# Scans that take their floor from a PSUM bank, one value accumulator in the first half, and half of a gate sum on ScalarE and POOL

## The chip, the cores and the metric

The kernel runs on one core of one Trainium2 chip. The metric is the device time of one execution in microseconds (us): 707.28 us, the median of three executions (706.64 to 707.72). Everything is fp32 at the interface. On the chip each matrix operand is split into a high and a low part (fp32r), and a product is made of three matmuls.

## The reference

One layer: adaptive LayerNorm of x (1024 x 1024), one projection into two groups of eight heads of 64, attention of two kinds, a SiLU gate, an output projection, and a residual with LayerNorm whose gate comes from a vector `c`. The two parts that the change touches:

```python
mod = jax.nn.silu(c) @ w_ada[layer] + b_ada[layer]
gate = mod[:, 2 * D_MODEL:]                      # the residual gate, 1024 numbers
...
def _stick_breaking_block(q, k, v, q_pos, k_pos):
    z = jnp.einsum('bhqd,bhkd->bhqk', q, k).astype(jnp.float32) * scale
    strict = k_pos[None, :] < q_pos[:, None]
    log_beta = jax.nn.log_sigmoid(z)
    log_keep = jnp.where(strict, jax.nn.log_sigmoid(-z), 0.0)
    later = lax.cumsum(log_keep, axis=3, reverse=True) - log_keep
    w = jnp.where(strict, jnp.exp(log_beta + later), 0.0)
    return jnp.einsum('bhqk,bhkd->bhqd', w.astype(v.dtype), v)
```

In words: the weight of key k for query q is sigmoid(z) at k times the product of sigmoid(-z) over the keys between k and q. The other group (forgetting attention) is an ordinary causal softmax.

## The kernel before, in words

**Stages.** The start (to about 96 us) normalises x, turns it (transposes on PE into PSUM tiles `xT`), and makes q, k and the gate `sg` for the first head pairs with accumulators `acc0` (first half of the columns) and `acc1` (second half); in between, `gate_term` (L690) sums the residual gate on VectorE (DVE): `gate += wg[kt] * sc[:, kt]`, eight terms, each in two halves of 512 columns. From 96 us on the attention runs over eight head pairs p = 0 to 7. Pairs 0 to 3 are stick-breaking, pairs 4 to 7 are softmax. A unit (p, h, i) is one head h and one block i of 128 queries against its `ke = (i + 1) * 128` keys. A pair has 16 units; in pairs 0 to 3 the block runs upward from 0 to 7 for each head, in pairs 4 to 6 downward, and in pair 7 the two heads alternate. Each unit goes through `att_scores` (S on PE at L410 and L411), two units later `att_transpose` (T on PE at L456, split into a high and a low part on ScalarE, L458, and DVE, L459), and after every second unit `att_pv` (L464), the product with the values. The next head pair's projections (`m`, L256 to L258; `v`, L311 to L313) are spread between the units as fillers. The tail is the output projection (`o`).

**A stick-breaking unit** in `att_scores`: ScalarE (ACT) makes `kp` = sigmoid(-S) and `be` = sigmoid(S) (L429, L430); the S tile has a single buffer, so the next unit's S waits for both. DVE then runs two scans from right to left over `kp`. A scan keeps a state: at each element, state = (data0 * state) op1 data1. The first (L434) goes over the 128 columns of the diagonal block with data1 = `ident` and op1 = max: the 1 of the identity starts the product at the diagonal, and its zeros keep what lies right of it at zero. The second (L437) goes over the `ke - 128` columns left of it, with data0 and data1 both `kp`, op1 = min, and starts from the last state. POOL multiplies `be` by the shifted `kp` (L439). Both scans read two streams from SBUF.

**The accumulators of `att_pv`.** `pv_tile` (L65) has two PSUM buffers with one tag, which all 64 products take in turn. After a product ACT copies one half of the rows (L490), DVE adds the other (L491), and POOL multiplies by the gate (L492).

**What sets the order.** PE's instructions stand in the order in which the program is written, and in the start SyncE's (SP) too. On DVE, ACT and POOL a scheduler orders instructions when the program is built; on the chip each engine then works through its own list in order. `after(...)` only holds a scheduled instruction behind others. [...]

Of the kernel before, what the change touches and what calls it, by code (L numbers as in the profile page):

```python
# [8 lines left out]
F32 = mybir.dt.float32  # L9
F32R = mybir.dt.float32r  # L10
AF = mybir.ActivationFunctionType
ALU = mybir.AluOpType

P = 128
# [13 lines left out]
def tile_hybrid_layer(  # L28
# [33 lines left out]
    def acc_tile(name):  # L62
        return ps.tile([P, 512], F32, tag="acc", bufs=2, name=name)

    def pv_tile(name):  # L65
        return ps.tile([P, 512], F32, tag="pv", bufs=2, name=name)

    def t_tile(name):
        return ps.tile([P, 512], F32, tag="T", bufs=2, name=name)
# [306 lines left out]


    st_w, st_pt = {}, {}

    zq = {}  # L380
    turn = [0, 0]
# [15 lines left out]
    def att_scores(u, following):  # L397
        p, h, i = u
        z = zq.pop(u)
        ke = (i + 1) * P  # L400
        ns = 1 if ke <= 512 else 2
        w = ke // ns
        qs = slice(i * P, i * P + P)
        dg = slice(ke - P, ke)
        if p >= 4:
            f = fb[2 * (p - 4) + h]
        S = s_tile(f"S_{p}_{h}_{i}")
        for s in range(ns):
            ks = slice(s * w, s * w + w)
            nc.tensor.matmul(S[:, s, :w], qst[p][h][:, qs], kst[p][h][:, ks], start=True, stop=False)  # L410
            nc.tensor.matmul(S[:, s, :w], z, klo[p][:, ks], start=False, stop=True)  # L411
        v3 = lambda a: a[:, :ke].rearrange("p (a b) -> p a b", a=ns)
        if p >= 4:
            a = att_tile(f"a_{p}_{h}_{i}")
            nm = sb.tile([P, 1], F32, tag="nm", bufs=4, name=f"nm_{p}_{h}_{i}")
            l = sb.tile([P, 1], F32, tag="l", bufs=4, name=f"l_{p}_{h}_{i}")
            nc.vector.tensor_tensor_reduce(out=v3(a), in0=S[:, :ns, :w], in1=v3(f),  # L417
                                           op0=ALU.add, op1=ALU.min, scale=-1.0, scalar=BIG,
                                           accum_out=nm)
            if following:  # L420
                att_causal(following)
            nc.scalar.activation(a[:, :ke], a[:, :ke], AF.Exp, scale=-1.0, bias=nm, accum_out=l)  # L422
            nc.vector.reciprocal(l, l)  # L423
            nc.gpsimd.tensor_scalar(a[:, :ke], a[:, :ke], l, 1.0, op0=ALU.mult, op1=ALU.mult)  # L424
            st_w[u] = a
        else:
            kp = att_tile(f"kp_{p}_{h}_{i}")
            be = att_tile(f"be_{p}_{h}_{i}")
            nc.scalar.activation(v3(kp), S[:, :ns, :w], AF.Sigmoid, scale=-1.0)  # L429
            nc.scalar.activation(v3(be), S[:, :ns, :w], AF.Sigmoid)  # L430


            rv = kp[:, dg][:, ::-1]
            nc.vector.tensor_tensor_scan(rv, rv, ident[:, ::-1], initial=0.0, op0=ALU.mult, op1=ALU.max)  # L434
            if i:
                rv = kp[:, :ke - P][:, ::-1]
                nc.vector.tensor_tensor_scan(rv, rv, rv, initial=kp[:, ke - P:ke - P + 1],  # L437
                                             op0=ALU.mult, op1=ALU.min)
            nc.gpsimd.tensor_tensor(be[:, :ke - 1], be[:, :ke - 1], kp[:, 1:ke], op=ALU.mult)  # L439
            nc.gpsimd.memset(be[:, ke - 1:ke], 0.0)  # L440
            st_w[u] = be
# [20 lines left out]
    y_last = []  # L462

    def att_pv(p, h, j):  # L464
        acc = pv_tile(f"pv_{p}_{h}_{j}")
        last = 2 * j + 1

        def product(part, kb, m=P, start=False, stop=False):
            pt = st_pt[p, h, j, kb // 4][part]
            q0 = P if kb == last else 0  # L470
            nc.tensor.matmul(acc[:m, q0:256], vt[p][:, kb, h * P:h * P + m], pt[:, kb % 4, q0:],  # L471
                             start=start, stop=stop)

        for kb in range(max(1, last - 1)):
            product(0, kb, start=kb == 0)
        product(0, last)
        for kb in range(last - 1):
            product(1, kb, HD)  # L480
        product(1, last, HD)
        if j:
            product(1, last - 1, HD)
        product(0 if j else 1, last - 1, stop=True)
        r = slice(h * HD, h * HD + HD)
        o = slice((1 - h) * HD, (1 - h) * HD + HD)
        qs = slice(j * 256, j * 256 + 256)
        ty = sb.tile([P, 512], F32, tag="ty", bufs=2, name=f"ty_{p}_{h}_{j}")
        tm, yt = ty[:, :256], ty[:, 256:]
        nc.scalar.copy(tm[r, :], acc[o, :256])  # L490
        nc.vector.tensor_tensor(yt[r, :], acc[r, :256], tm[r, :], op=ALU.add)  # L491
        nc.gpsimd.tensor_tensor(yt[r, :], yt[r, :], sgt[p][r, qs], op=ALU.mult)  # L492
        if p == NPAIR - 1:
            if not y_last:
                y_last.extend([big("sg", 2, "y7h", F32R), big("kl", 2, "y7l", F32R)])
            yh, yl = y_last
            nc.scalar.copy(yh[r, qs], yt[r, :])
            nc.gpsimd.tensor_tensor(yl[r, qs], yt[r, :], yh.bitcast(F32)[r, qs], op=ALU.subtract)
        else:
            nc.sync.dma_start(y_dr[p, r, qs], yt[r, :])  # L500
# [15 lines left out]
    START = ((0, 0), (0, 1), (0, 2), (1, 0), (1, 1))  # L516
    NW = 4
    xt_early = t_tile("xT_early")
    acc0 = [t_tile("st_q0"), acc_tile("st_k0"), acc_tile("st_g0"), pv_tile("st_q1"), pv_tile("st_k1")]
    raw_w, split, split_at, used = {}, {}, {}, [0]  # L520
    raws = []

# [167 lines left out]
    def gate_term(kt, h):  # L690
        s = slice(h * 512, h * 512 + 512)
        if kt == 0:
            nc.vector.tensor_scalar(gate[:, s], wg[kt][:, s], sc[:, 0:1], None, op0=ALU.mult)
        else:
            nc.vector.scalar_tensor_tensor(gate[:, s], wg[kt][:, s], sc[:, kt:kt + 1], gate[:, s],
                                           op0=ALU.mult, op1=ALU.add)
# [34 lines left out]
    for kb in range(NB):  # L731
# [5 lines left out]
        if kb < len(evacs):  # L737
            n, h = evacs[kb]
            with after(*rounded):
                evac_m(*START[n], 0, acc0[n], (h,))  # L740
    acc1 += [pv_tile("st_g0b"), pv_tile("st_q1b"), acc_tile("st_k1b")]
    v0_w.update((n, fetch_w(f"v0_{n}b", w_v[0, n], 512)) for n in (2, 3))
    for n in range(5):
        if n >= 2:
            for kb in range(NB):
                start_steps((n,), acc1, kb, 512, 1024)
                step = (n - 2) * NB + kb
                if step % 3 == 1 and step // 3 < GEARLY:
                    with after(rounded[1]):
                        gate_term(step // 3, 0)  # L750
                        gate_term(step // 3, 1)
                    if step // 3 < 4:
                        load_gate(step // 3 + 4)
        last_evac = evac_m(*START[n], 1, acc1[n])
    bf_sb = cp.tile([P, 8], F32, tag="bf", name="bf_sb")
    nc.sync.dma_start(bf_sb, b_f.to_broadcast([P, 8]))
    start_order.__exit__(None, None, None)
# [279 lines left out]
```

## Time and profile before

| | before |
|---|---|
| median of 3 runs | 707.28 us |
| the profiled execution's own time | 706.96 us |
| its span in the profile | 705.2 us |
| granted TensorE clock, mean | 0.997 |
| PE, DVE, ACT, POOL busy | 678.0, 513.8, 378.6, 421.6 us |

"Busy" is the time in which an engine had an instruction; an idle time is put down to the instruction that released the engine (the releaser). The views used below are the page's groups, the groups by shape, the waits of one engine, the timeline of one engine (start, duration, engine, line, names; in brackets the idle time before the row and its releaser) and a table by stretch. 1.76 us of the execution's time lie outside the span.

### The profile page before, as it was taken

Reading aid. Unit: us, or ns where it says so; the run is one execution under the profiler, and the core shown is the slowest. Engines: PE = TensorE matmul, PEld = TensorE weight load, DVE = VectorE, ACT = ScalarE, POOL = GpSimd, SP = SyncE. Lnnn points to the kernel's source line nnn. Section 1 sums busy time; section 2 is a strip of 40 time slices with the busy share of each in tenths; the row PEclk is TensorE's granted clock in tenths of the full one; section 3 lists DMA queues with packets and bytes.
Section 4 is the critical chain, followed back from the end, with each engine's and each line's share of the span. In section 5 each row is a group of like instructions: output and inputs, shape, how many; then the busy total and the mean of one; then the engine's idle time right before and its main releaser. Section 6 shows DMA issues by size and latency. Waiting matters only on the chain.

```text
span 705.2 us, 11790 instructions
## 1 busy us (share of the span) xinstructions
PE 678.0 (96%) x4033; PEld 589.7 (84%) x4033; DVE 513.8 (73%) x963; ACT 378.6 (54%) x856; POOL 421.6 (60%) x523
## 2 busy tenths in 40 slices
PE   7999998989999999999999999999999999999995
PEld 4789887878898888889988887889988889888884
DVE  5985689897858697788686684759576767784644
ACT  4667346756658566666665554645564667621000
POOL 4560258665629675857368898858574455665412
PEclk9999999999999999999999999999999999999998
DMA  8953451102101212112044654435251189143301
GB/s 306 416 211 126 128 172 35 28 26 53 53 7 36 71 37 68 42 38 68 9 124 126 201 162 131 148 104 170 71 170 53 56 268 374 43 159 122 121 32 59
DMA packets 44027, 81.59 MB, mean 116 GB/s; under 512 B 5120, under 2 KB 18880, under 8 KB 43072
## 3 DMA queue, kind: packets, MB, share of 16 engines
q1 hardware_dynamic: 42816, 76.65, 32.9%
q10 hardware_dynamic: 1152, 4.19, 2.1%
q8 instruction: 32, 0.52, 0.3%
q14 instruction: 27, 0.22, 0.1%
HBM read 60.34 MB, written 16.29 MB: 109 GB/s over the span
## 4 chain that ended last, share of the span: by engine, by line
PE 54%; DVE 3%; POOL 3%; DMA 2%; issue 1%; ACT 1%; POOLq 0%; SPq 0%; DVEq 0%; ACTq 0%
PE pv L471 6%; PE m L256 6%; PE m L257 6%; PE m L258 6%; PE T L456 6%; PE o L825 4%; PE o L823 4%; PE o L824 4%; PE S L410 3%; PE S L411 3%; PE v L311 2%; PE v L313 2%; PE v L312 2%; DMA fb<-f_dr 1%; DVE kp L437 1%
## 5 line engine op out<-in xcount | busy, mean ns | idle before, releaser
L256 PE MATMUL m<-uh,whi 128*128 128x512 f32 x304 | 126.3, 416 | 0.8 <-DVE kl L244 0.8
L257 PE MATMUL m<-ul,whi 128*128 128x512 f32 x304 | 119.8, 394 | 0.0
L258 PE MATMUL m<-uh,wlo 128*128 128x512 f32 x304 | 119.6, 394 | 0.0
L459 DVE TENSOR_TENSOR pt<-T,pt 128x512 fp32r<-128x512 f32 (+2 forms) x192 | 100.5, 549 | 14.8 <-ACT pt L458 13.5
L439 POOL TENSOR_TENSOR be<-be,kp 128x127 f32<-128x127 f32 (+3 forms) x64 | 79.1, 1236 | 48.6 <-DVE kp L437 45.9
L458 ACT CAST pt<-T 128x512 fp32r<-128x512 f32 (+2 forms) x192 | 85.7, 480 | 18.7 <-PE T L456 15.3
L471 PE MATMUL pv<-pt,v 128*128 128x256 f32 (+3 forms) x640 | 82.9, 273 | 6.2 <-DVE pt L459 5.4
L471 PEld LDWEIGHTS pv<-pt,v 128*128 128x128 f32 (+1 forms) x640 | 77.6, 163 | 12.5 <-DVE pt L459 7.1
L437 DVE TENSOR_TENSOR_SCAN kp<-kp 128x128 f32<-128x128 f32 (+6 forms) x56 | 83.0, 1483 | 1.9
L424 POOL TENSOR_SCALAR a<-a,l 128x1024 f32<-128x1024 f32 (+3 forms) x64 | 48.4, 756 | 41.7 <-DVE l L423 29.5
L422 ACT ACTIVATE a<-a,nm 128x1024 f32<-128x1024 f32 (+3 forms) x64 | 49.8, 778 | 40.0 <-DVE nm L417 39.2
L410 PE MATMUL S<-k,q 128*128 128x512 f32 (+5 forms) x192 | 66.6, 348 | 2.4 <-ACT be L430 1.7
L258 PEld LDWEIGHTS m<-uh,wlo 128*128 128x128 f32 x304 | 57.1, 188 | 13.5
L411 PE MATMUL S<-kl,qz 128*128 128x512 f32 (+5 forms) x192 | 65.5, 342 | 0.0
L256 PEld LDWEIGHTS m<-uh,whi 128*128 128x128 f32 x304 | 57.3, 188 | 9.6 <-DVE kl L244 1.2
L257 PEld LDWEIGHTS m<-ul,whi 128*128 128x128 f32 x304 | 57.4, 189 | 7.9
L434 DVE TENSOR_TENSOR_SCAN kp<-kp,ident 128x128 f32<-128x128 f32 x64 | 42.5, 665 | 24.6 <-ACT kp L429 22.9
L492 POOL TENSOR_TENSOR ty<-ty,sg 64x256 f32<-64x256 f32 x64 | 49.3, 771 | 18.5 <-DVE ty L491 8.8
L429 ACT ACTIVATE kp<-S 128x128 f32<-128x128 f32 (+3 forms) x64 | 41.7, 652 | 32.2 <-PE S L411 30.7
L417 DVE CUSTOM_DVE_ANT_0 a<-S,fb 128x1024 f32<-128x1024 f32 (+3 forms) x64 | 48.3, 754 | 14.5 <-PE S L411 5.9
L126 POOL TENSOR_TENSOR wlo<-raw,whi 128x512 fp32r<-128x512 f32 x38 | 56.6, 1492 | 2.4 <-DMA wo_dr<-wlo_o 0.8
L311 PE MATMUL v<-whi_v,uh 128*128 128x256 f32 (+1 forms) x192 | 56.1, 292 | 1.2 <-DVE kl L244 1.2
(280 smaller groups left out, 1637.5 us busy)
## 6 DMA issues: line engine op xcount, KB each, us to landing
raw<-in_w_qkg_dram SPq DMA_DIRECT2D x38, 256.0 KB, 3.0
wss<-in_w_ss_dram SPq DMA_DIRECT2D x7, 1024.0 KB, 8.3
x<-in_x_dram SPq DMA_DIRECT2D x8, 512.0 KB, 7.7
k<-k SPq DMA_DIRECT2D x32, 128.0 KB, 2.2
wg<-in_w_gate_dram SPq DMA_DIRECT2D x8, 512.0 KB, 5.0
raw_o<-in_w_out_dram SPq DMA_DIRECT2D x16, 256.0 KB, 2.7
fb<-f_dr ACTq DMA_DIRECT2D x8, 512.0 KB, 4.3
wo_dr<-whi_o SPq DMA_DIRECT2D x16, 256.0 KB, 2.8
```

Of the source, the lines that this page charges most:

```text
L126: nc.gpsimd.tensor_tensor(lo[:, :n], raw, hi.bitcast(F32)[:, :n], op=ALU.subtract)
L256: nc.tensor.matmul(acc, hi[:, c], u_hi[kt][:, s], start=(kt == 0), stop=False)
L257: nc.tensor.matmul(acc, hi[:, c], u_lo[kt][:, s], start=False, stop=False)
L258: nc.tensor.matmul(acc, lo[:, c], u_hi[kt][:, s], start=False, stop=(kt == NB - 1))
L311: nc.tensor.matmul(acc[:, :n], u_hi[kt][:, ts_], hi[:, s], start=(kt == 0), stop=False)
L410: nc.tensor.matmul(S[:, s, :w], qst[p][h][:, qs], kst[p][h][:, ks], start=True, stop=False)
L411: nc.tensor.matmul(S[:, s, :w], z, klo[p][:, ks], start=False, stop=True)
L437: nc.vector.tensor_tensor_scan(rv, rv, rv, initial=kp[:, ke - P:ke - P + 1], op0=ALU.mult, op1=ALU.min)
L439: nc.gpsimd.tensor_tensor(be[:, :ke - 1], be[:, :ke - 1], kp[:, 1:ke], op=ALU.mult)
L458: nc.scalar.copy(hi[:, :n, qo:qo + P], t3)
L459: nc.vector.tensor_tensor(lo[:, :n, qo:qo + P], t3, hi.bitcast(F32)[:, :n, qo:qo + P], op=ALU.subtract)
L471: nc.tensor.matmul(acc[:m, q0:256], vt[p][:, kb, h * P:h * P + m], pt[:, kb % 4, q0:], start=start, stop=stop)
```

## The change

Four edits. A PSUM bank with the tag `fl` holds a tile `floor` during the first half: zeros in columns 0 to 383 and the identity in columns 384 to 511 (written once, at the end of the start, by DVE and ACT). The scans of a unit take data1 from it: one scan of up to 512 columns that covers the diagonal block and the blocks left of it, and, where `ke` is over 512, a second one over the rest whose data1 is the first column of `floor`, broadcast (zeros), with op1 = max. The bank comes from the second `pv` buffer: `att_pv` has one buffer in pairs 0 to 3, and from pair 4 on the two banks in turn by j. In pair 7, where the heads alternate, two products that follow each other then have the same j and so the same bank. The accumulators of the start that took two `pv` buffers take `pv` and `fl`. Last, the first term of the residual gate goes to ACT, and for the first 512 columns of the other seven ACT scales the weight tile in place and POOL adds it to `gate`; the second 512 columns stay on DVE. Both are now held behind both instructions of `rounded`.

```diff
-    def pv_tile(name):
-        return ps.tile([P, 512], F32, tag="pv", bufs=2, name=name)
+    def pv_tile(name, other=False):
+        return ps.tile([P, 512], F32, tag="fl" if other else "pv", bufs=1, name=name)
...
-            rv = kp[:, dg][:, ::-1]
-            nc.vector.tensor_tensor_scan(rv, rv, ident[:, ::-1], initial=0.0, op0=ALU.mult, op1=ALU.max)
-            if i:
-                rv = kp[:, :ke - P][:, ::-1]
-                nc.vector.tensor_tensor_scan(rv, rv, rv, initial=kp[:, ke - P:ke - P + 1],
-                                             op0=ALU.mult, op1=ALU.min)
+            n = min(ke, 512)
+            rv = kp[:, ke - n:ke][:, ::-1]
+            nc.vector.tensor_tensor_scan(rv, rv, floor[0][:, 512 - n:][:, ::-1], initial=0.0,
+                                         op0=ALU.mult, op1=ALU.max)
+            if ke > n:
+                rv = kp[:, :ke - n][:, ::-1]
+                nc.vector.tensor_tensor_scan(rv, rv, floor[0][:, 0:1].to_broadcast([P, ke - n]),
+                                             initial=kp[:, ke - n:ke - n + 1], op0=ALU.mult, op1=ALU.max)
...
-        acc = pv_tile(f"pv_{p}_{h}_{j}")
+        acc = pv_tile(f"pv_{p}_{h}_{j}", p >= 4 and j % 2 == 1)
...
-    acc0 = [t_tile("st_q0"), acc_tile("st_k0"), acc_tile("st_g0"), pv_tile("st_q1"), pv_tile("st_k1")]
+    acc0 = [t_tile("st_q0"), acc_tile("st_k0"), acc_tile("st_g0"), pv_tile("st_q1"), pv_tile("st_k1", True)]
...
         if kt == 0:
-            nc.vector.tensor_scalar(gate[:, s], wg[kt][:, s], sc[:, 0:1], None, op0=ALU.mult)
+            nc.scalar.activation(gate[:, s], wg[kt][:, s], AF.Copy, scale=sc[:, 0:1])
+        elif h == 0:
+            nc.scalar.activation(wg[kt][:, s], wg[kt][:, s], AF.Copy, scale=sc[:, kt:kt + 1])
+            nc.gpsimd.tensor_tensor(gate[:, s], gate[:, s], wg[kt][:, s], op=ALU.add)
         else:
             nc.vector.scalar_tensor_tensor(gate[:, s], wg[kt][:, s], sc[:, kt:kt + 1], gate[:, s],
                                            op0=ALU.mult, op1=ALU.add)
...
-    acc1 += [pv_tile("st_g0b"), pv_tile("st_q1b"), acc_tile("st_k1b")]
+    acc1 += [pv_tile("st_g0b", True), pv_tile("st_q1b"), acc_tile("st_k1b")]
...
-                    with after(rounded[1]):
+                    with after(*rounded):
                         gate_term(step // 3, 0)
                         gate_term(step // 3, 1)
...
+        if n == 2:
+            floor.append(ps.tile([P, 512], F32, tag="fl", bufs=1, name="floor"))
+            nc.vector.memset(floor[0][:, :512 - P], 0.0)
+            nc.scalar.copy(floor[0][:, 512 - P:], ident)
```

What the change moves on the engines is seen at three places. In these lists a row is line, operation, output<-inputs and size of the output; a scan is listed there as SCALAR_TENSOR_TENSOR. PE's order is the same before and after, and DVE's differs only where scans and gate terms come and go.

The first place is DVE at the end of the start. `q` and `kl` are evacuations of the start's accumulators `st_q1b` and `st_k1b`, `wg_831` to `wg_872` the weight tiles of the gate's last four terms. Before:

```order
L695 SCALAR_TENSOR_TENSOR gate<-wg_831,sc,gate 128x512 x2
L695 SCALAR_TENSOR_TENSOR gate<-wg_844,sc,gate 128x512
L233 SCALAR_TENSOR_TENSOR q_0_251<-st_q1b,q_0_251 64x512
L695 SCALAR_TENSOR_TENSOR gate<-wg_844,sc,gate 128x512
L695 SCALAR_TENSOR_TENSOR gate<-wg_857,sc,gate 128x512
L233 SCALAR_TENSOR_TENSOR q_1_252<-st_q1b,q_1_252 64x512
L695 SCALAR_TENSOR_TENSOR gate<-wg_857,sc,gate 128x512
L695 SCALAR_TENSOR_TENSOR gate<-wg_872,sc,gate 128x512 x2
L244 TENSOR_TENSOR kl_255<-st_k1b,k_0_253 64x512
```

The same place on DVE after the change (the weight tiles are numbered 831, 845, 859 and 878 there):

```order
L763 MEMSET floor 128x384
L701 SCALAR_TENSOR_TENSOR gate<-wg_831,sc,gate 128x512
L701 SCALAR_TENSOR_TENSOR gate<-wg_845,sc,gate 128x512
L233 SCALAR_TENSOR_TENSOR q_0_251<-st_q1b,q_0_251 64x512
L701 SCALAR_TENSOR_TENSOR gate<-wg_859,sc,gate 128x512
L233 SCALAR_TENSOR_TENSOR q_1_252<-st_q1b,q_1_252 64x512
L701 SCALAR_TENSOR_TENSOR gate<-wg_878,sc,gate 128x512
L244 TENSOR_TENSOR kl_255<-st_k1b,k_0_253 64x512
```

Ahead of `kl` stand one gate term where there were three; four of eight terms in this stretch left DVE, and the memset of `floor` came.

The second place is POOL over the same time and into the first units. `whi` and `wlo` are the splits of the weights of the fillers, `be` the product of a unit. Before:

```order
L125 TENSOR_SCALAR whi_2_0_1217<-raw_2_0_1215 128x512
L126 TENSOR_TENSOR wlo_2_0_1218<-raw_2_0_1215,whi_2_0_1217 128x512
L125 TENSOR_SCALAR whi_2_1_1223<-raw_2_1_1221 128x512
L126 TENSOR_TENSOR wlo_2_1_1224<-raw_2_1_1221,whi_2_1_1223 128x512
L440 MEMSET be_0_0_941 128x1
L439 TENSOR_TENSOR be_0_0_941<-be_0_0_941,kp_0_0_940 128x127
```

After the change, on POOL:

```order
L699 TENSOR_TENSOR gate<-gate,wg_831 128x512
L699 TENSOR_TENSOR gate<-gate,wg_845 128x512
L699 TENSOR_TENSOR gate<-gate,wg_859 128x512
L125 TENSOR_SCALAR whi_2_0_1224<-raw_2_0_1222 128x512
L699 TENSOR_TENSOR gate<-gate,wg_878 128x512
L125 TENSOR_SCALAR whi_2_1_1230<-raw_2_1_1228 128x512
L126 TENSOR_TENSOR wlo_2_0_1225<-raw_2_0_1222,whi_2_0_1224 128x512
L126 TENSOR_TENSOR wlo_2_1_1231<-raw_2_1_1228,whi_2_1_1230 128x512
L443 MEMSET be_0_0_951 128x1
L442 TENSOR_TENSOR be_0_0_951<-be_0_0_951,kp_0_0_950 128x127
```

Four additions stand ahead of the first unit's `be` that were not on POOL before (three more stand further ahead).

The third place is DVE in two units of the first head, blocks 5 and 6. `pt` is the low part of a turned block, `ty` the evacuation of a product. Before:

```order
L434 SCALAR_TENSOR_TENSOR kp_0_5_1124<-kp_0_5_1124,ident 128x128
L437 SCALAR_TENSOR_TENSOR kp_0_5_1124<-kp_0_5_1124 128x640
L708 SCALAR_TENSOR_TENSOR gate<-bg,gate_1146 128x512
L459 TENSOR_TENSOR pt_0_0_1_0_1112<-T_0_3_0_1149,pt_0_0_1_0_1111 128x4x128
L434 SCALAR_TENSOR_TENSOR kp_0_6_1161<-kp_0_6_1161,ident 128x128
L437 SCALAR_TENSOR_TENSOR kp_0_6_1161<-kp_0_6_1161 128x768
```

After the change, on DVE:

```order
L436 SCALAR_TENSOR_TENSOR kp_0_5_1131<-kp_0_5_1131,floor 128x512
L440 SCALAR_TENSOR_TENSOR kp_0_5_1131<-kp_0_5_1131,floor 128x256
L714 SCALAR_TENSOR_TENSOR gate<-bg,gate_1153 128x512
L462 TENSOR_TENSOR pt_0_0_1_0_1119<-T_0_3_0_1156,pt_0_0_1_0_1118 128x4x128
L436 SCALAR_TENSOR_TENSOR kp_0_6_1168<-kp_0_6_1168,floor 128x512
L440 SCALAR_TENSOR_TENSOR kp_0_6_1168<-kp_0_6_1168,floor 128x384
```

The scans keep their places between the same neighbours; 128 + 640 columns became 512 + 256, and units of up to 512 keys have one scan instead of two.

More of the change, by code (lines that the diff above doesn't have):

```diff
@@ L378, in tile_hybrid_layer @@
     st_w, st_pt = {}, {}
+    floor = []
     zq = {}
```

## The prediction

> **What bounds the kernel now.** I read the page's busy times first, then a table by stretch, then the waits of PE.
>
> ```profile
> span 705.2 us, 11790 instructions
> PE 678.0 (96%) x4033; PEld 589.7 (84%) x4033; DVE 513.8 (73%) x963; ACT 378.6 (54%) x856; POOL 421.6 (60%) x523
> 96.00:365.00 269.00, 258.82 (x1667) 231.96 (x1667) 215.57 (x327) 173.23 (x392) 175.10 (x217) 1.00 0.18 51
> ```
>
> PE is the bound: busy 96% of the span at a full clock. The last row is the stick-breaking half, 96 to 365 us; its columns are the length, then the busy time of PE, weight loads, DVE, ACT and POOL, the clock and DMA. The change touches the end of the start and this half. There PE is idle for only 269.00 - 258.82 = 10.2 us, so whatever DVE saves, no more than about that can come back. Who holds PE in that stretch (from 95 us, so that the first wait is whole):
>
> ```profile
> PE pv L471 <- DVE pt L459: 3.7, 6, 1.3
> PE S L410 <- ACT be L430: 1.7, 1, 1.7
> PE T L456 <- POOL wlo_v L126: 1.6, 1, 1.6
> PE T L456 <- DVE pt L459: 1.3, 1, 1.3
> PE v L311 <- DVE kl L244: 1.2, 1, 1.2
> PE pv L471 <- ACT pt L458: 0.7, 1, 0.7
> PE T L456 <- POOL be L440: 0.2, 1, 0.2
> ```
>
> The rows sum to 10.4 us. DVE ends 3.7 + 1.3 + 1.2 = 6.2 us of them directly. A wait is somewhat longer than its row says, because a matmul's end is modelled:
>
> ```profile
> 92.20 0.40 PE L565 MATMUL st_k1b<-uh,hw 128*128 128x512 f32 x1
> 92.44 0.39 PE L568 MATMUL st_k1b<-ul,hw 128*128 128x512 f32 x1
> ```
>
> The second starts 0.24 us after the first, whose row lasts 0.40. So each of the 12 waits hides about 0.16 us more: 1.9 us, and the whole prize is about 12.3 us.
>
> **The scans.** Their durations by line (minimum/median/maximum in ns), beside the DVE operation that splits the turned blocks:
>
> ```profile
> L434 DVE TENSOR_TENSOR_SCAN kp<-kp,ident x64: 406/427/1954, 97.8 to 360.3; 128x128 f32<-128x128 f32 x64
> L459 DVE TENSOR_TENSOR pt<-T,pt x192: 259/608/693, 102.0 to 644.9; 128x512 fp32r<-128x512 f32 x96, 128x128 fp32r<-128x128 f32 x32, 128x256 fp32r<-128x256 f32 x32, 128x384 fp32r<-128x384 f32 x32
> ```
>
> L434 is one shape, and yet lasts from 0.41 to 1.95 us. L459 reads one stream from PSUM and one from SBUF, and in 192 runs never exceeds 0.693 us. What stretches a scan is POOL at work, and POOL is stretched too:
>
> ```profile
> 117.16 2.94 DVE L437 TENSOR_TENSOR_SCAN kp<-kp 128x896 f32<-128x896 f32 x1
> 118.17 3.49 POOL L439 TENSOR_TENSOR be<-be,kp 128x895 f32<-128x895 f32 x1
> 120.02 0.99 DVE L459 TENSOR_TENSOR pt<-T,pt 128x512 fp32r<-128x512 f32 x2
> 120.74 0.99 PE L471 MATMUL pv<-pt,v 128*64 128x256 f32 x7 [1.29 <-DVE pt L459]
> ```
>
> Here the chain is whole: a long scan overlaps POOL's product, the split of T stands behind the scan in DVE's list, and PE waits 1.29 us. The new scans read `kp` from SBUF and data1 from PSUM, two streams of the same kinds as L459's, so I take them undisturbed. Undisturbed scans, and the sums of all of them from the page:
>
> ```profile
> 331.83 0.42 DVE L434 TENSOR_TENSOR_SCAN kp<-kp,ident 128x128 f32<-128x128 f32 x1
> 332.29 0.48 DVE L437 TENSOR_TENSOR_SCAN kp<-kp 128x128 f32<-128x128 f32 x1
> 345.59 1.28 DVE L437 TENSOR_TENSOR_SCAN kp<-kp 128x512 f32<-128x512 f32 x1
> L437 DVE TENSOR_TENSOR_SCAN kp<-kp 128x128 f32<-128x128 f32 (+6 forms) x56 | 83.0, 1483 | 1.9
> L434 DVE TENSOR_TENSOR_SCAN kp<-kp,ident 128x128 f32<-128x128 f32 x64 | 42.5, 665 | 24.6 <-ACT kp L429 22.9 <-ACT qz L388 1.0
> L437 DVE TENSOR_TENSOR_SCAN kp<-kp 128x896 f32<-128x896 f32 x8 | 20.4, 2556 | 0.3
> ```
>
> From 128 to 512 columns an undisturbed scan grows by 0.80 us, 2.08 ns a column. A first scan then takes 0.42, 0.69, 0.95 and 1.22 us for 128 to 512 columns, and a second (it starts from a value in SBUF) 0.48, 0.75, 1.02 and 1.28. Over the eight blocks of a head that is 0.42 + 0.69 + 0.95 + 5 x 1.22 + 0.48 + 0.75 + 1.02 + 1.28 = 11.7 us; times eight heads 93.5 us, where the two rows show 83.0 + 42.5 = 125.5. DVE is relieved of **32 us**, 0.5 us a unit. No row shows a scan fed from PSUM. Its bounds: not cheaper than one column per step of L459 (512 columns in about 0.69 us, so 8 x 6.7 = 53 us over all), not dearer than now, 125.5, unless PSUM feeds it more slowly than it feeds L459 (a rival below). I take 93.5, from the nearest rows. All scans keep their places in DVE's list.
>
> [...]
>
> **The gate's terms.** The first wait of 1.7 us comes from them:
>
> ```profile
> 92.27 3.46 DVE L695 SCALAR_TENSOR_TENSOR gate<-wg,sc,gate 128x512 f32<-128x512 f32 x3
> 95.76 0.68 DVE L244 TENSOR_TENSOR kl<-st_k1b,k 64x512 fp32r<-64x512 f32 x1
> 96.48 0.58 ACT L241 CAST k<-st_k1b 64x512 fp32r<-64x512 f32 x1 [2.83 <-DVE kl L244]
> 97.26 0.27 ACT L430 ACTIVATE be<-S 128x128 f32<-128x128 f32 x1
> 97.58 0.38 PE L410 MATMUL S<-k,q 128*128 128x256 f32 x1 [1.67 <-ACT be L430]
> ```
>
> Three terms (3.46 us) hold `kl` until 95.76, that holds ACT's second copy of k, which holds `be`, and the second unit's S waits. After the change one term stands there, about 1.2 us at this rate. ACT's first copy still ends near 93.45, so `kl` can run at 93.5, ACT's `be` ends near 95.3, and PE, whose fillers last until 95.9, does not wait: **-1.7 us**. What the moved work costs elsewhere:
>
> ```profile
> L123 POOL TENSOR_TENSOR raw_o<-raw_o,gate 128x512 f32<-128x512 f32 x16 | 20.7, 1294 | 8.8 <-DMA raw_o<-in_w_out_dram 8.6
> L552 ACT CAST whi_st<-raws 128x512 fp32r<-128x512 f32 x5 | 2.9, 616 | 1.2 <-DMA raws<-in_w_qkg_dram 1.2
> L695 DVE SCALAR_TENSOR_TENSOR gate<-wg,sc,gate x14: 743/748/1773, 75.3 to 94.0; 128x512 f32<-128x512 f32 x14
> 82.44 0.62 POOL L125 TENSOR_SCALAR whi_v_2b<-raw_v_2b 128x512 fp32r<-128x512 f32 x1 [29.98 <-PE st_q1b L568]
> 87.28 0.59 ACT L232 ACTIVATE q<-st_q1b 64x512 fp32r<-64x512 f32 x1 [4.39 <-PE st_q1b L568]
> 92.57 0.93 POOL L125 TENSOR_SCALAR whi<-raw 128x512 fp32r<-128x512 f32 x1 [6.29 <-DMA raw<-in_w_qkg_dram]
> 98.33 0.41 POOL L439 TENSOR_TENSOR be<-be,kp 128x127 f32<-128x127 f32 x1 [0.64 <-DVE kp L434]
> 99.74 0.27 PE L456 MATMUL T<-ident,be 128*128 128x128 f32 x1
> ```
>
> ACT gets nine instructions of about 0.62 us (L552 has the shape), 5.6 us, in idle time such as the 4.39 us ahead of 87.28; bounds 0.59 and 0.75 us each change nothing there. The floor's two writes (no row shows a memset into PSUM; between 0.1 and 0.7 us, as an L459 of 512 columns) fall before 87 us, where DVE also has nothing to do. POOL gets seven additions at 1.3 us (L123), bounded by 0.74, the cheapest term on DVE, and 3.5 us, the stretched product above. Three fall into the 29.98 us of idle time ahead of 82.44. The gate's last four weight tiles land only shortly before the raw weights that POOL awaits at 92.57, so one addition falls behind that row and delays the two splits and the first `be` with it: 92.57 + 0.9 (split) + 1.3 (addition) + 0.6 + 2 x 1.3 (splits) + 0.5 = 98.5 to 98.7 at the end of `be`, as before. PE wants it at 99.74 - 1.7 = 98.1: a new wait of **+0.5 us**, up to 3 if the additions stretch, nothing if they run at the lower bound.
>
> **One accumulator in the first half.** A product may start only when ACT and DVE have read the one before. The tightest case:
>
> ```profile
> 112.67 0.99 PE L471 MATMUL pv<-pt,v 128*128 128x256 f32 x8
> 115.30 0.40 DVE L491 TENSOR_TENSOR ty<-pv,ty 64x256 f32<-64x256 f32 x1
> 118.70 0.75 PE L471 MATMUL pv<-pt,v 128*128 128x256 f32 x5
> ```
>
> It is read out at 115.70 and the next product begins at 118.70: 3.0 us of slack, and every other product of the timeline leaves more, those of pair 7 too. With scans shorter, DVE's read comes earlier. **0 us**; if it bit, a tenth of a microsecond a product would be 3 us. Behind the waiting product stand T, S and the fillers of the next unit, which is why it would count in full.
>
> **The sum.** Beside the first wait (-1.7 + 0.5): of the 5.0 us in which PE waits for `pt`, four fifths go, since DVE gains 0.5 us a unit cumulatively while it is behind and 0.9 in a long one (3.46 us for the pair at 117 becomes 2.50); -4.0. Of the remaining 3.7 us (`kl`, POOL's split, ACT's `pt`, `be`) I take 60%, because POOL's products start after the scans and are no longer stretched by them, and `kl` stands behind scans, while ACT and the order of POOL's list stay; -2.2. Hidden parts go in the same proportion, 7.4 of 10.4, of 1.9 us: -1.4. Together -8.8 us. The profiled execution took 706.96 us (span 705.2 and 1.76 around it), so 698.2; it lay 0.3 us under the median, so **698.5 us**. The second half keeps its work, starts earlier and is PE-bound.
>
> **Rivals.** (1) *POOL takes over.* The first half's waits move from DVE to POOL: it gets 9 us more just ahead of the attention, and one wait already ends at its split (1.6 us). The first and POOL's waits then stay: half the gain, 4.4 us, 702.9 us. Against it: POOL is idle for 94 of 269 us and mostly waits for scans. [...] (3) *The waits only change their names*, within 0.2% (1.4 us), about what a measurement can tell from no change. (4) *Slower: PSUM feeds a scan more slowly than SBUF.* A unit has (269.00 - 215.57) / 64 = 0.83 us of idle DVE. The longest pair now takes 0.67 + 2.56 = 3.2 us in the mean (L434, and L437 of 896 columns); the rival decides once it costs over 4.0 us, 1.6 times my 2.5. At twice my cost a long unit is 1.0 us over, and 32 long units add some 20 us after the gate's relief: about 720 us. For it only that no row shows such a scan; against it L459, at full rate.
>
> **Chances.** Forecast 0.70; rival 1 0.14; rival 2 0.05; rival 3 0.04; rival 4 0.07. Faster 0.89, same 0.04, slower 0.07. If every wait goes, 12.3 us, the time is 695.0, and 1.5 us more for gaps too short to be listed give the low end, 693.5; rival 1 with a larger POOL price gives the high end, 704.0.
>
> **What would show it.** Right: scans at 0.42 to 1.28 us with a maximum near the median; no product on POOL near 3.5 us; DVE some 35 us less busy; no wait for `be` near 96; PE's idle in the first half down from 10 to about 3 us. Wrong: scans of over 1.3 us for 512 columns (rival 4), or of scattered length (rival 2); PE's waits ended by POOL (rival 1); a product that waits for L491's successor (the accumulator).

## The result, and the profile after

| | before | after |
|---|---|---|
| median | 706.96 us of 4 runs (706.30 to 707.72) | 699.11 us of 4 runs (698.09 to 699.99) |
| the profiled execution, its span | 706.96, 705.2 us | 699.99, 698.2 us |

The ratio is 0.9888, with a 95% interval of 0.9871 to 0.9905: the kernel became 1.1% faster, 7.85 us, and the forecast of 698.5 us lies 0.6 us under the median. The sections behind this one show that its term for the gate nevertheless failed, and that it left out a wait.

First the busy times of the page, then the stick-breaking half in the table by stretch (length; busy time of PE, weight loads, DVE, ACT, POOL; clock; DMA), for the kernel after:

```profile
span 698.2 us, 11781 instructions
PE 676.0 (97%) x4033; PEld 589.0 (84%) x4033; DVE 483.7 (69%) x931; ACT 385.0 (55%) x866; POOL 410.6 (59%) x530
96.00:365.00 269.00, 264.10 (x1710) 237.65 (x1710) 191.15 (x314) 177.94 (x398) 163.06 (x224) 1.00 0.19 51
```

PE's idle time in that stretch fell from 10.2 to 269.00 - 264.10 = 4.9 us. DVE is 30.1 us less busy over the span, and POOL 11.0 us less, though it got seven additions more. The waits of PE from 92 to 365 us, in the kernel after (us in total, times, longest):

```profile
PE pv L474 <- DVE pt L462: 2.0, 2, 1.6
PE T L459 <- POOL be L443: 1.1, 1, 1.1
PE T L459 <- DVE pt L462: 1.0, 2, 0.9
PE S L411 <- ACT be L431: 0.8, 1, 0.8
PE v L311 <- DVE kl L244: 0.7, 1, 0.7
```

Twelve waits of 10.4 us became seven of 5.6. Two of the seven are new: the 1.1 us for POOL's `be`, which the prediction had at 0.5, and one of 1.6 us for `pt`, which it did not have. Three of the prediction's signs came out weaker: PE's idle time (about 3 us forecast), DVE (about 35 us less busy forecast) and the first wait for `be`, which is shorter but not gone.

The scans and POOL's product, by line (ns, minimum/median/maximum), and the scans of one shape (busy us, mean ns), in the kernel after:

```profile
L440 DVE TENSOR_TENSOR_SCAN kp<-kp,floor x32: 479/880/1281, 105.7 to 355.4; 128x128 f32<-128x128 f32 x8, 128x256 f32<-128x256 f32 x8, 128x384 f32<-128x384 f32 x8, 128x512 f32<-128x512 f32 x8
L442 POOL TENSOR_TENSOR be<-be,kp x64: 402/1204/2002, 98.7 to 356.7; 128x127 f32<-128x127 f32 x8, 128x255 f32<-128x255 f32 x8, 128x383 f32<-128x383 f32 x8, 128x511 f32<-128x511 f32 x8
L436 DVE TENSOR_TENSOR_SCAN kp<-kp,floor 128x512 f32<-128x512 f32 x40 | 48.8, 1219 | 25.6 <-ACT kp L430 24.9 <-issue 0.5
L436 DVE TENSOR_TENSOR_SCAN kp<-kp,floor 128x128 f32<-128x128 f32 x8 | 3.3, 410 | 0.0
L436 DVE TENSOR_TENSOR_SCAN kp<-kp,floor 128x512 f32<-128x512 f32 (+2 forms) x64 | 65.2, 1018 | 32.4 <-ACT kp L430 31.4
```

A scan of one shape now has one duration, to 0.02 us within each shape of the two lines: 1.22 us for 512 columns where 1.22 was forecast (1.20 to 1.22 in 40 scans), 0.41 for 128 where 0.42 was (0.40 to 0.42 in 8). All of L436 and L440 together are 65.2 + 28.1 = 93.3 us (28.1 is 32 times the mean of the four forms, 0.88), against a forecast of 93.5. POOL's product, before up to 3.49 us, is never over 2.00. A scan and a product side by side, DVE and then POOL, in the kernel after:

```profile
115.74 1.22 DVE L436 TENSOR_TENSOR_SCAN kp<-kp,floor 128x512 f32<-128x512 f32 x1
117.00 1.28 DVE L440 TENSOR_TENSOR_SCAN kp<-kp,floor 128x512 f32<-128x512 f32 x1
115.61 1.77 POOL L442 TENSOR_TENSOR be<-be,kp 128x895 f32<-128x895 f32 x1
```

The first scan lies wholly inside POOL's product, and neither is stretched: the scan takes the mean of its shape, and the product 1.77 us, where the same 895 columns took 3.49 beside a scan before.

**Where the time came from.** The starts of the S rows cut the first half into stages that repeat from run to run to about 0.1 us outside stage A (where the start differs). A is the first head of pair 0 (from its first S to the first S of the second head), B goes on to the first S of pair 2, C to the second head of pair 4, when the last stick-breaking unit is through. Worked out from those rows for the kernels of this study, one profile each; "rest" is what remains of the span (the start and everything behind C):

| us | A | B | C | A+B+C | rest |
|---|---|---|---|---|---|
| before | 25.9 | 103.9 | 177.9 | 307.7 | 397.5 |
| after | 25.8 | 99.3 | 176.2 | 301.3 | 396.9 |
| scans only | 27.1 | 99.3 | 176.2 | 302.6 | 397.3 |
| gate only | 26.6 | 104.0 | 177.9 | 308.5 | 395.4 |
| one accumulator only | 27.3 | 103.9 | 177.9 | 309.1 | 397.0 |
| smaller first scan | 25.6 | 99.3 | 176.2 | 301.1 | 397.5 |
| second scan from SBUF | 26.5 | 100.6 | 178.2 | 305.3 | 398.6 |
| gate term late | 25.9 | 99.3 | 176.2 | 301.5 | 395.9 |
| logarithms late | 25.6 | 99.3 | 174.5 | 299.3 | 396.4 |
| `be` first | 24.4 | 99.3 | 176.2 | 299.9 | 397.1 |
| both | 24.3 | 99.3 | 174.5 | 298.1 | 396.4 |

The change wins 6.4 us in A to C, nothing of it in A, where the gate was to pay. The rest scatters between 395.4 and 398.6 us without regard to the scans; of the 1.5 us of the 7.85 that A to C do not explain, 0.6 lie in it, and 0.9 come from the profiled execution of the change being the slowest of its four. Neither is traced further.

### The profile page after: what moved, and what is told of

The parts are those of the page before. It is cut to its first block, busy times and chain, and to the rows that moved or that the text cites. A ratio compares the mean times of both kernels' runs of the same rounds, so it can differ in the third digit from the quotient of the medians.

```text
span 698.2 us, 11781 instructions
## 1 busy us (share of the span) xinstructions
PE 676.0 (97%) x4033; PEld 589.0 (84%) x4033; DVE 483.7 (69%) x931; ACT 385.0 (55%) x866; POOL 410.6 (59%) x530
## 4 chain that ended last, share of the span: by engine, by line
PE 76%; DVE 7%; DMA 5%; POOL 4%; ACT 4%; issue 3%; SPq 0%; POOLq 0%; DVEq 0%; ACTq 0%
PE pv L474 9%; PE m L256 8%; PE m L257 8%; PE m L258 8%; PE T L459 8%; PE o L835 4%; PE o L833 4%; PE o L834 4%; PE S L412 4%; PE S L411 4%; PE v L311 3%; PE v L313 3%; PE v L312 3%; DMA wss<-in_w_ss_dram 1%; DMA raw<-in_w_qkg_dram 1%
## 5 line engine op out<-in xcount | busy, mean ns | idle before, releaser
L462 DVE TENSOR_TENSOR pt<-T,pt 128x512 fp32r<-128x512 f32 (+2 forms) x192 | 100.6, 550 | 16.1 <-ACT pt L461 14.9
L442 POOL TENSOR_TENSOR be<-be,kp 128x127 f32<-128x127 f32 (+3 forms) x64 | 77.1, 1205 | 34.9 <-DVE kp L440 25.9
L436 DVE TENSOR_TENSOR_SCAN kp<-kp,floor 128x512 f32<-128x512 f32 (+2 forms) x64 | 65.2, 1018 | 32.4 <-ACT kp L430 31.4
L495 POOL TENSOR_TENSOR ty<-ty,sg 64x256 f32<-64x256 f32 x64 | 47.7, 745 | 26.5 <-DVE ty L494 12.5
L389 ACT CAST qz<-q 64x128 fp32r<-64x128 f32 x128 | 37.4, 295 | 31.3 <-PE S L412 30.0
L313 PE MATMUL v<-wlo_v,uh 128*128 128x256 f32 (+1 forms) x192 | 54.2, 282 | 0.0
```

The lines of the kernel that those rows point to most:

```text
L313: nc.tensor.matmul(acc[:, :n], u_hi[kt][:, ts_], lo[:, s], start=False, stop=(kt == NB - 1))
L436: nc.vector.tensor_tensor_scan(rv, rv, floor[0][:, 512 - n:][:, ::-1], initial=0.0, op0=ALU.mult, op1=ALU.max)
L462: nc.vector.tensor_tensor(lo[:, :n, qo:qo + P], t3, hi.bitcast(F32)[:, :n, qo:qo + P], op=ALU.subtract)
```

## The experiments

**1. The scans without the gate.** The change with all gate terms back on DVE, held as they were before:

```diff
-            nc.scalar.activation(gate[:, s], wg[kt][:, s], AF.Copy, scale=sc[:, 0:1])
-        elif h == 0:
-            nc.scalar.activation(wg[kt][:, s], wg[kt][:, s], AF.Copy, scale=sc[:, kt:kt + 1])
-            nc.gpsimd.tensor_tensor(gate[:, s], gate[:, s], wg[kt][:, s], op=ALU.add)
+            nc.vector.tensor_scalar(gate[:, s], wg[kt][:, s], sc[:, 0:1], None, op0=ALU.mult)
```

> The change without its gate part (the eight terms stay on DVE). My theory: the scans' feed carries most of the 7.9 us; the gate part is worth the first wait of 1.7 us less the 0.5 to 1.1 us of POOL's new wait, so this kernel loses 0.6 to 1.5 us of the gain: about 700.2 us, and PE again waits about 1.7 us for be near 96 us. Rival (the gate part is the gain): over 703 us.

699.93 us (6 runs; before 706.64 of 23 on that chip), ratio 0.9901, interval 0.988 to 0.9923. The scans alone carry the gain, as far as the intervals tell. PE's wait for `be` is back, at 1.82 us, and A is 1.2 us longer than before, with PE's clock at 0.50 from 97.53 to 100.92 us behind that wait (see the last section). A is also 1.3 us longer than in the change, though the change waits as long in two parts (0.78 + 1.11 us); what the gate part gains beside the new scans is, in these two profiles, the clock.

**2. The gate without the scans.** The kernel before with the new `gate_term` and its `after` alone.

> The kernel before with the gate part alone. My theory: 0.6 to 1.7 us faster than before, about 705.8 us; scans still scattered up to 2 or 3 us, DVE busy some 5 us less, the waits of PE at 115 to 150 us as before. Rival (the gate part is the gain): 702 us or less.

706.89 us (12 runs), ratio 1.0001, interval 0.9989 to 1.0013: no effect, where 0.6 to 1.7 us were expected. The two waits of PE that matter, in this kernel:

```profile
95.62 0.39 PE L410 MATMUL S<-k,q 128*128 128x256 f32 x1 [0.54 <-ACT be L430]
99.35 0.33 PE L456 MATMUL T<-ident,be 128*128 128x128 f32 x1 [1.42 <-POOL be L440]
```

0.54 + 1.42 = 1.96 us stand where 1.67 stood: the wait moved from ACT's `be` to POOL's.

**3. One accumulator alone.** The kernel before with `pv_tile` of the change and no floor.

> The kernel before with one value accumulator in the first half and the two banks by j later; nothing else. My theory: no difference, within 0.7 us of before, and no product that waits for ACT's or DVE's read of the one before. Rival (the single accumulator costs and the scans pay for it): 1 to 3 us slower.

707.67 us (12 runs), ratio 1.0017, interval 1.0002 to 1.0031. That is 1.0 us more than before, beyond the 0.7 expected. No product waits for an accumulator in the list of waits, and B and C are those of before, 103.9 and 177.9 us. The 1.4 us more in A stand behind a gap of 1.78 us, where PE's clock fell to 0.50 for 3.4 us (last section). The mean clock is under 0.996 in nine of its 12 executions, in eight of the 23 of the kernel before. So the clock carries the difference as far as these figures go; whether the edit lengthens that gap (1.67 us before) is not shown.

**4. Smaller scans from the same bank.** With `n = P` in place of `n = min(ke, 512)` the first scan takes 128 columns only, and the number of scans is that of before; all read PSUM.

> The change with its first scan cut to the 128 columns of the diagonal, as before, and the rest in the second, both fed from PSUM: as many scans as before, undisturbed. My theory (the second stream's place is what counts): within 1 us of the change, 699.1 to 700.0 us, no scan more than a few ns from its median, DVE some 5 us busier than in the change. Rival (fewer instructions are what counts): half the gain lost, 703 us or more.

699.63 us (6 runs), ratio 0.9896, interval 0.988 to 0.9913, like the change. DVE is busy 487.4 us, 3.7 more, and PE's waits are those of the change to 0.3 us. So the gain does not come from fewer or merged scans.

**5. The change again**, beside the next two and on the same chip (before 706.90 of 17 runs).

> The changed kernel itself, for a narrower interval on the chip of the next three: 7.0 to 8.5 us faster than before by every theory.

699.25 us (5 runs), ratio 0.9891, interval 0.9872 to 0.991.

**6. The second scan from SBUF.** The scans keep their number and sizes, but the second one, of 32 units out of 64, reads `kp` as data1 again:

```diff
-                nc.vector.tensor_tensor_scan(rv, rv, floor[0][:, 0:1].to_broadcast([P, ke - n]),
-                                             initial=kp[:, ke - n:ke - n + 1], op0=ALU.mult, op1=ALU.max)
+                nc.vector.tensor_tensor_scan(rv, rv, rv,
+                                             initial=kp[:, ke - n:ke - n + 1], op0=ALU.mult, op1=ALU.min)
```

> The change with its second scan fed from SBUF twice, as before (kp as data1, min); the first keeps its floor in PSUM. The number of scans and their columns are those of the change. My theory: the 32 second scans stretch again beside POOL, up to 2 us, first scans stay at 1.22; 1.5 to 4 us of the gain are lost, about 701.5 us. Rival (fewer and merged scans are the gain): no difference from the change.

705.17 us (12 runs), ratio 0.9977, interval 0.9963 to 0.9991. 5.9 of the 7.65 us that the change gains on that chip are gone, more than expected. The same line and two of PE's waits, in this kernel:

```profile
L440 DVE TENSOR_TENSOR_SCAN kp<-kp x32: 484/1018/2407, 105.9 to 359.5; 128x128 f32<-128x128 f32 x8, 128x256 f32<-128x256 f32 x8, 128x384 f32<-128x384 f32 x8, 128x512 f32<-128x512 f32 x8
116.60 0.63 PE L459 MATMUL T<-ident,be 128*128 128x128 f32 x4 [1.83 <-DVE pt L462]
224.28 0.98 PE L474 MATMUL pv<-pt,v 128*64 128x256 f32 x7 [2.57 <-DVE pt L462]
```

The minimum of L440 stays (484 ns beside 479), its maximum goes from 1281 to 2407, and PE waits longer for DVE's split: 1.83 us at 116.60, where the longest such wait of T is 0.9 in the kernel after, and 2.57 at 224.28. The latter is not a scan's: it is the new wait of 1.64 us, grown because the first of the two small steps of experiment 8 takes 1.93 us here, where 1.23 in the change. That the second stream comes from PSUM is what the gain rests on: with the shapes kept, taking it away in a third of the scans gives most of the gain back. A to C account for 4.0 us of the loss, of which that wait is 0.9. The rest of this profile is 398.6 us, with a wait of 2.24 us at 445 us for POOL, whose list waits 1.45 us for the output weights' transfers at 445.13; whether the edit causes it, one profile does not tell. So how much of the 5.9 us the scans alone cost is not separated.

**7. The last gate term later.** The change with gate term 8 written behind the last evacuation of the start, to take its addition off POOL's list ahead of `be`.

> The change with the gate's eighth term written behind the last evacuation of the start and held behind it. My theory: what is left of the waits near 95 and 98 us (0.8 for be on ACT, 1.1 for be on POOL) comes from that term on DVE and POOL; the first goes and the second shrinks to half or less: 0.8 to 1.4 us faster than the change. Rival (the weight splits on POOL hold the first product anyway): the first wait goes and the second grows by as much; same time as the change.

699.12 us (5 runs), ratio 0.9894, interval 0.9872 to 0.9916: the same. POOL's list in this kernel, and the T that waits:

```profile
94.23 1.21 POOL L125 TENSOR_SCALAR whi<-raw 128x512 fp32r<-128x512 f32 x2
95.39 3.00 POOL L126 TENSOR_TENSOR wlo<-raw,whi 128x512 fp32r<-128x512 f32 x2
98.36 1.26 POOL L699 TENSOR_TENSOR gate<-gate,wg 128x512 f32<-128x512 f32 x1
99.61 0.41 POOL L442 TENSOR_TENSOR be<-be,kp 128x127 f32<-128x127 f32 x1
100.07 0.33 PE L459 MATMUL T<-ident,be 128*128 128x128 f32 x1 [1.74 <-POOL be L443]
```

The scheduler put the addition behind the splits and still ahead of `be`. S waits only 0.26 us now, but T 1.74. So the experiment did not clear POOL's list, and the rival was right that it only renames the wait. The list shows what to move instead: the splits, 1.21 + 3.00 us for the weight "1_2", which PE needs later.

**8. The forget gate's logarithms behind the split.** This goes for the new wait of 1.64 us at 220.85 us. DVE, POOL and PE there, in the kernel after:

```profile
217.69 1.23 DVE L346 SCALAR_TENSOR_TENSOR flf<-fsb,fab 128x64 f32<-128x64 f32 x1 [0.94 <-ACT fab L345]
218.95 1.26 DVE L349 TENSOR_TENSOR_SCAN fsb<-flf,later 128x64 f32<-128x64 f32 x1
220.13 0.99 DVE L462 TENSOR_TENSOR pt<-T,pt 128x512 fp32r<-128x512 f32 x2
216.84 2.00 POOL L442 TENSOR_TENSOR be<-be,kp 128x1023 f32<-128x1023 f32 x1 [0.47 <-DVE kp L440]
218.79 2.51 POOL L126 TENSOR_TENSOR wlo<-raw,whi 128x512 fp32r<-128x512 f32 x2
220.85 0.98 PE L474 MATMUL pv<-pt,v 128*64 128x256 f32 x7 [1.64 <-DVE pt L462]
```

And the same two steps with POOL's rows around them, in the kernel before:

```profile
224.49 0.23 DVE L346 SCALAR_TENSOR_TENSOR flf<-fsb,fab 128x64 f32<-128x64 f32 x1 [0.30 <-ACT fab L345]
224.75 0.60 DVE L349 TENSOR_TENSOR_SCAN fsb<-flf,later 128x64 f32<-128x64 f32 x1
222.40 2.21 POOL L125 TENSOR_SCALAR whi<-raw 128x512 fp32r<-128x512 f32 x1
225.19 2.00 POOL L439 TENSOR_TENSOR be<-be,kp 128x1023 f32<-128x1023 f32 x1
```

Two steps of 64 columns took 0.23 and 0.60 us before, when POOL had been held up by a long scan (896 columns, 2.38 us from 221.82; POOL's cast at 222.40 takes 2.21 us, where 0.62 is the median of its line) and came to its product late. After the change POOL is on time, its two-stream operations run from 216.84 to 221.30 without a break, and the two steps, each with two tiles of SBUF, take 1.23 and 1.26. The first ends at 218.92, 0.08 us after POOL's product; the second at 220.21, about when the first of the two `wlo` is through (218.79 and half of 2.51: 220.05). In experiment 6 the first takes 1.93 us, from 220.42, and again ends 0.08 us after POOL's product (222.27). That POOL stretches them is read from these rows; no kernel gave one of their inputs a place in PSUM. The experiment holds both behind the split:

```diff
-        nc.vector.scalar_tensor_tensor(lf, ff, 0.0, ab, op0=ALU.min, op1=ALU.subtract)
+        for _ in range(FLATE):
+            yield
+        with after(last_split[0]):
+            nc.vector.scalar_tensor_tensor(lf, ff, 0.0, ab, op0=ALU.min, op1=ALU.subtract)
...
-            nc.vector.tensor_tensor(lo[:, :n, qo:qo + P], t3, hi.bitcast(F32)[:, :n, qo:qo + P],
-                                    op=ALU.subtract)
+            last_split[0] = nc.vector.tensor_tensor(lo[:, :n, qo:qo + P], t3,
+                                                    hi.bitcast(F32)[:, :n, qo:qo + P], op=ALU.subtract)
```

> The change, with the two last steps of the forget gate's logarithms (the minimum and the running sum, 64 columns each) put behind the split of T that they stand ahead of on VectorE near 217.7 us. Theory: in the change these two take 1.23 and 1.26 us because they read two tiles of SBUF while POOL multiplies and splits, and the split and PE's product wait behind them; with the split ahead of them, PE's wait of 1.64 us at 220.85 falls under 0.5 us, the two steps still last over 1 us each but nobody waits, and the time is 1.1 to 1.6 us below the change (0.9984 of it or less). Rival: the split waits for T or for ScalarE's copy anyway, so the wait keeps at least 1 us under another name and the time stays within 0.5 us of the change.

697.65 us (4 runs; before 706.14 of 9 on that chip, for the last four experiments), ratio 0.9871, interval 0.9852 to 0.989; the change itself took 699.64 beside it. The 1.99 us are more than the 1.1 to 1.6 expected, and all runs (697.43 to 698.03) lie below those of the change (698.74 to 700.07). DVE in this kernel:

```profile
218.06 1.02 DVE L467 TENSOR_TENSOR pt<-T,pt 128x512 fp32r<-128x512 f32 x2 [1.41 <-ACT pt L466]
219.00 1.07 DVE L353 SCALAR_TENSOR_TENSOR flf<-fsb,fab 128x64 f32<-128x64 f32 x1
220.10 1.28 DVE L354 TENSOR_TENSOR_SCAN fsb<-flf,later 128x64 f32<-128x64 f32 x1
```

The split runs at 218.06 in place of 220.13, PE's wait is gone, and C is 1.7 us shorter. The two steps still take 1.07 and 1.28 us, and nobody waits for them. The overlap was not removed but moved to where it is free, as the theory had it.

**9. `be` ahead of the splits.** The change with POOL's splits of the weight "1_2" held behind the first unit's product:

```diff
+        with after(*(first_be if key[:3] == "1_2" else ())):
+            nc.gpsimd.tensor_scalar(hi[:, :n], raw, 1.0, 1.0, op0=ALU.mult, op1=ALU.mult)
+            nc.gpsimd.tensor_tensor(lo[:, :n], raw, hi.bitcast(F32)[:, :n], op=ALU.subtract)
...
+            held = nc.gpsimd.tensor_tensor(be[:, :ke - 1], be[:, :ke - 1], kp[:, 1:ke], op=ALU.mult)
...
+            if not first_be:
+                first_be.append(held)
```

> The change, with POOL's two weight splits near 93.3 to 98.7 us held behind the first unit's product be. Theory: the wait of 1.11 us for be that the change brought in is POOL's queue (two splits and one gate addition ahead of be); without the splits ahead of it be can run at about 96.5 us, PE's wait at 98.1 goes, and the time is 0.8 to 1.3 us below the change. Rival: the wait only moves on: the splits then stand between the first products, the second or third unit's T waits for its be by about as much, and the time stays within 0.5 us of the change.

698.02 us (5 runs), ratio 0.9876, interval 0.9857 to 0.9894; 1.62 us under the change, where 0.8 to 1.3 were expected. POOL's list, in this kernel:

```profile
92.26 3.00 POOL L704 TENSOR_TENSOR gate<-gate,wg 128x512 f32<-128x512 f32 x2 [1.06 <-ACT wg L703]
96.69 0.41 POOL L445 TENSOR_TENSOR be<-be,kp 128x127 f32<-128x127 f32 x1 [0.63 <-DVE kp L439]
97.07 1.20 POOL L126 TENSOR_SCALAR whi<-raw 128x512 fp32r<-128x512 f32 x2
98.86 2.55 POOL L127 TENSOR_TENSOR wlo<-raw,whi 128x512 fp32r<-128x512 f32 x2
```

`be` waits for its scan now, not for POOL, and runs 2 us earlier. T has no wait, A is 24.4 us, 1.4 less than in the change, and no later product waits in its place.

**10. Both.**

> Both of the above in one kernel. Theory: the two waits are apart in time and add: 2 to 2.8 us below the change, a ratio to the kernel before of 0.985 to 0.986. Rival: one of the two does nothing, and the time is that of the other alone.

695.89 us (5 runs, 695.27 to 696.50), ratio 0.9845, interval 0.9825 to 0.9864. The stretch and the waits of PE from 92 to 365 us, in this kernel:

```profile
96.00:365.00 269.00, 266.84 (x1724) 240.17 (x1724) 193.67 (x320) 180.15 (x402) 166.46 (x226) 1.00 0.19 53
PE T L469 <- DVE pt L472: 0.9, 1, 0.9
PE v L315 <- DVE kl L248: 0.7, 1, 0.7
PE S L419 <- ACT be L439: 0.6, 1, 0.6
PE pv L484 <- DVE pt L472: 0.4, 1, 0.4
```

The two gains add (1.99 + 1.62 = 3.61): 3.75 us under the change on the same chip, where 2 to 2.8 were expected. PE idles 2.2 us in the stretch, and this version is faster than both kernels.

**11. The change once more**, beside the last three.

> The change itself, for comparison on the same chip: 698.6 to 699.9 us, a ratio of 0.988 to 0.990.

699.64 us (5 runs), ratio 0.9896, interval 0.9878 to 0.9913.

## Why the prediction was right, point by point, and where not

**The bound and the prize: right.** "The whole prize", it says, "is about 12.3 us": with the two mends (experiment 10) the stages A to C are 307.7 - 298.1 = 9.6 us shorter than before, and waits of 2.6 us are left in the list.

**The scans: right.** 93.3 us for 93.5, so 32.2 us less on DVE, where 32 were forecast. That DVE as a whole fell by only 30.1, where about 35 were forecast, goes with other steps that take longer now: the seven gate terms left on it 1.25 us in the mean, where the fourteen of before took 0.85, and the two small steps of experiment 8 together 2.49 us, where 0.83. That a stream from PSUM takes the scans out of POOL's way is shown by experiments 4 and 6 together: with the number of scans of before and all of them fed from PSUM the time is 699.63 us, with the number of the change and a third of them fed from SBUF alone it is 705.17 and the longest of these lasts 2.41 us in place of 1.28. What counts is where the second stream comes from, not the number of scans. The scattered lengths that were the sign for rival 2 are gone, and rival 4 falls too: the scan of 128 columns takes 410 ns in the mean, where an undisturbed one from SBUF took 0.42 us. How POOL and DVE hold each other up was not shown, only by how much: a product of 895 columns took 3.49 us beside a scan with two streams from SBUF, and takes 1.77 beside one with its second stream from PSUM.

**The waits for `pt`: right for the old ones.** Of the 5.0 us, 4.0 were to go. In the list after there are 2.0 + 1.0 = 3.0 us, of which 1.64 are the new wait; 1.4 of the old are left, so 3.6 went.

**The rest: somewhat too low.** Of 3.7 us, 2.2 were to go; only `kl` is left with 0.7, so 3.0 went. POOL's split, which held T for 1.6 us, is gone from the list with the new scans alone (experiment 1) and stays in it with the gate or the accumulator alone (2 and 3): it was the scans that made POOL late.

**The gate's terms: the term that was mis-sized.** It was put at -1.7 + 0.5. The first two waits sum to 0.78 + 1.11 = 1.89 us after, where 1.67 stood, and the gate alone measured a ratio of 1.0001. The step that failed is "one addition falls behind that row". On POOL, in the kernel after, with the rows ahead of `be`:

```profile
92.06 1.31 POOL L699 TENSOR_TENSOR gate<-gate,wg 128x512 f32<-128x512 f32 x1 [1.06 <-ACT wg L698]
93.33 1.07 POOL L125 TENSOR_SCALAR whi<-raw 128x512 fp32r<-128x512 f32 x1
94.37 1.27 POOL L699 TENSOR_TENSOR gate<-gate,wg 128x512 f32<-128x512 f32 x1
98.73 0.41 POOL L442 TENSOR_TENSOR be<-be,kp 128x127 f32<-128x127 f32 x1
```

Two additions of 1.3 us come after 92 us, the first already at the place of the cast, and `be` ends at 99.14, not at 98.5 to 98.7. The other half of the term, that S would not wait, failed by 0.8 us, and for two reasons. ACT's `be` was late:

```profile
92.31 1.61 DVE L701 SCALAR_TENSOR_TENSOR gate<-wg,sc,gate 128x512 f32<-128x512 f32 x1
95.45 0.27 ACT L431 ACTIVATE be<-S 128x128 f32<-128x128 f32 x1
94.71 0.28 PE L313 MATMUL v<-wlo_v_3b,uh 128*128 128x256 f32 x1
95.78 0.38 PE L411 MATMUL S<-k,q 128*128 128x256 f32 x1 [0.78 <-ACT be L431]
```

The DVE term left there ran beside POOL's addition and took 1.61 us where 1.2 was put in, so `kl` ran at 93.95 instead of 93.5, and `be` ended at 95.72 instead of near 95.3. And PE was early: its fillers lasted until 94.99, not 95.9, because its first S came at 91.75, where 92.67 before. That start varies by execution: in experiment 5, with a first S at 92.54, the same wait is 0.45 us. The mechanism of rival 1 (POOL's list) is real at this place, and rival 3 (the waits only change their names) describes the gate part alone. Experiment 9 shows that moving the two splits is enough; what taking the additions away would give was not measured.

**What was not in it: a wait of 1.64 us at 220.85 us.** The prediction let POOL's operations come earlier and asked only who waits for them, not whom they block. Two small DVE steps outside the scans also read two SBUF streams, and POOL's earlier work fell on them: they took 0.23 and 0.60 us before and take 1.23 and 1.26 after. Experiment 8 shows that PE's wait hangs on these two steps: with the split ahead of them the wait goes and 2 us with it. That POOL is what stretches them is read from the rows there.

**The sum.** The forecast had -8.8 us in the first half. Measured were -6.4: the gate's 1.2 us and the hidden part of it did not come, the new wait took 1.8 with its hidden part, and the scans brought somewhat more than put in. That the median came within 0.6 us of the forecast is in part luck: it is owed to the 1.5 us outside the stages, which no term explains.

**One accumulator: right for the products.** No product waits for one, and experiment 3 leaves B and C as they were; whether the edit has a part in the longer A there stays open.

## What to carry to other kernels

Where DVE and POOL both work on SBUF, look for DVE instructions with two SBUF inputs whose durations scatter within one shape (here 0.41 to 1.95 us for 128 columns), and try a place in PSUM for one of the inputs; equal shapes with equal durations (here 0.40 to 0.42) then show that it worked. After such a relief search the list for small instructions of the same kind that POOL now meets elsewhere (here one went from 0.23 to 1.23 us), and put what PE waits for ahead of them (1.99 us in experiment 8). Work that is moved to another engine must be placed in that engine's list by what stands behind it: an idle share over a stretch says nothing of the one product that PE waits for (POOL was idle for 105.9 of 269 us after the change, and PE waited 1.11 us for its `be`).

## What the hardware showed that was not expected

PE's granted clock fell to 0.50 for 3.4 us behind some gaps in its work, in three profiles. PE's row behind the gap and the table by stretch (the clock is the third value from the right), in the kernel with one accumulator only:

```profile
97.17 0.38 PE L410 MATMUL S<-k,q 128*128 128x256 f32 x1 [1.78 <-ACT be L430]
97.20:97.46 0.26, 0.26 (x2) 0.26 (x3) 0.23 (x2) 0.08 (x1) 0.07 (x1) 1.00 0.80 158
97.48:100.88 3.40, 3.40 (x18) 3.30 (x16) 1.90 (x5) 0.99 (x4) 2.92 (x5) 0.50 0.57 140
100.90:101.50 0.60, 0.60 (x7) 0.60 (x6) 0.00 (x0) 0.48 (x2) 0.10 (x1) 1.00 0.07 10
```

The clock is still 1.00 when PE goes on at 97.17, 0.50 from 97.48 to 100.88, and 1.00 again behind that. Half of 3.4 us is 1.7 us of PE's work, about as much as the gap; stage A is 1.4 us longer there than before. The same followed the gap of 1.82 us at 95.3 us with the scans only (0.50 from 97.53 to 100.92) and the one of 2.24 us at 445 us in experiment 6 (0.50 from 447.68 to 451.07). In the kernel before, the gap of 1.67 us at the same place was followed by 1.00, and in experiment 6 so were the ones of 1.83 us before 116.60 and of 2.57 us before 224.28. So some gaps of 1.78 us or more cost the clock and others do not, and which ones is open; it was not tried.

One thing more can be read: the fall comes when PE has gone on, and not at one fixed time behind the gap. PE goes on at 97.17 us with one accumulator and the clock is 0.50 from 97.48, 0.31 us later; with the scans only it is 0.43 us (97.10 and 97.53), in experiment 6 it is 0.11 (447.57 and 447.68). What sets the moment of the fall was not shown.
